# Row sums of a 64 MB tensor: the last row in a tile of its own, its first part's sum passed on as an element and not as a start value

## The chip, the cores and the metric

The kernel runs on one core of one Trainium2 chip. The metric is device microseconds of one execution. Every run that is told here is marked as fast in the record, with a granted clock (the share of the full clock that the chip allowed) of 1.0.

## The reference

```python
def setup_inputs():
    batch, seq, dim = 32, 512, 1024
    return {
        "x": np.random.randn(batch, seq, dim).astype(np.float32),
        "multiplier": 0.5,
    }

def reference(x, multiplier):
    return (np.sum(x, axis=-1) * multiplier).astype(np.float32)
```

There are 16384 rows of 1024 fp32 numbers, 67.11 MB in all. Each row becomes one number.

## The kernel before

The 128 partitions take 128 rows each. Seven blocks of 16 rows per partition are loaded whole, 8 MB at a time; the last block comes in pieces of 8, 5 and 2 rows, and its last row in two parts of 576 and 448 elements. This keeps the work that must follow the last byte small. In the last block, VectorE adds one half of a row to the other and sums as it goes, so that the size of such a sum is counted in pairs of elements. In the seven blocks before, it reduces whole rows and multiplies the results by 0.5. ScalarE takes some of the rows.

```python
    part = res_pool.tile([P, 1], fp32, name="part")
    # ...
    def dve_span(t, r, lo, hi, dst, start=0.0):
        mid = (lo + hi) // 2
        return nc.vector.tensor_tensor_reduce(
            out=t[:, r, lo:mid],
            in0=t[:, r, lo:mid],
            in1=t[:, r, mid:hi],
            scale=mul,
            scalar=start,          # the sum starts from this
            op0=ADD,
            op1=ADD,
            accum_out=dst,
        )
    # ... the last row of the last block
    for lo, hi in ((0, cut), (cut, D)):          # cut = 576, D = 1024
        loads.append(nc.sync.dma_start(
            out=t[:, B - 1, lo:hi], in_=x_last[:, B - 1, lo:hi]))
    # ...
    first = dve_span(t, B - 1, 0, cut, part)
    part_seen = nop_after(nc.vector, [first], [])     # waits until part is written
    final = dve_span(t, B - 1, cut, D, res[:, rows - 1 : rows], start=part)
    # ... store of the last 16 results of each partition, which waits for final
```

The sum of the first part goes into `part`, one number per partition. The sum of the second part starts from it. Two things must be true before that second sum may start: its load has landed, and `part` is written. The first wait is in the instruction; the second has a no-op of its own in front.

## Time and profile before

| | before |
|---|---|
| time, median of 3 runs | 161.98 us (161.96 to 161.98) |
| span of the trace | 160.2 us |
| transfer engines, busy | 97.4% |
| VectorE, busy | 74% |
| last load landed | 157.467 us |
| last sum, from start to end | 157.551 to 158.001 us |

The table is to be read from its third line: the transfers are the limit, and only what comes after the last landing is in the hands of the compute engines. The prediction shows the lines. Times to the nanosecond, here and below, are from the trace's records of instructions and of semaphore counts; 0 is the start of the span. A semaphore is a counter that instructions wait for, and the count of a load is complete when its sixteenth increment is there. In the profile's lines DVE is VectorE, DVEq its queue, SPq the queue that issues the transfers, and CUSTOM_DVE_ANT_0 the fused add and sum.

### The profile page before, as it was taken

Reading aid. Unit: us, or ns where it says so; the run is one execution under the profiler, and the core shown is the slowest. Engines: PE = TensorE matmul, PEld = TensorE weight load, DVE = VectorE, ACT = ScalarE, POOL = GpSimd, SP = SyncE. Lnnn points to the kernel's source line nnn. Section 1 sums busy time; section 2 is a strip of 40 time slices with the busy share of each in tenths; the row PEclk is TensorE's granted clock in tenths of the full one; section 3 lists DMA queues with packets and bytes.
Section 4 is the critical chain, followed back from the end, with each engine's and each line's share of the span. In section 5 each row is a group of like instructions: output and inputs, shape, how many; then the busy total and the mean of one; then the engine's idle time right before and its main releaser. Section 6 shows DMA issues by size and latency. Waiting matters only on the chain.

```text
span 160.2 us, 138 instructions
## 1 busy us (share of the span) xinstructions
DVE 119.3 (74%) x34; ACT 17.3 (11%) x31; POOL 0.2 (0%) x4
## 2 busy tenths in 40 slices
DVE  0000059997799969999599995999959999597443
ACT  0000000000000000000000000000000000599952
POOL 0000000000000000000000000000000000000000
DMA  7996996996996996997997998979969969999992
GB/s 278 507 524 262 524 524 262 524 524 262 524 524 262 524 524 262 524 475 311 524 442 344 524 409 376 524 311 475 524 278 507 524 278 507 393 393 425 430 399 72
DMA packets 2016, 67.18 MB, mean 419 GB/s; under 512 B 480, under 2 KB 608, under 8 KB 736
## 3 DMA queue, kind: packets, MB, share of 16 engines
q1 hardware_dynamic: 2016, 67.18, 97.4%
HBM read 67.11 MB, written 0.07 MB: 419 GB/s over the span
## 4 chain that ended last, share of the span: by engine, by line
DMA 75%; DVE 22%; SPq 1%; issue 0%; DVEq 0%
DMA xb<-in_x_dram 75%; DVE sums L96 22%; SPq L114 1%; DVE xb L80 0%; SPq L120 0%; SPq L94 0%; DVE res L99 0%; DVEq L205 0%
## 5 line engine op out<-in xcount | busy, mean ns | idle before, releaser
L96 DVE TENSOR_REDUCE sums<-xb 128x16 f32<-128x16384 f32 (+1 forms) x7 | 112.0, 16001 | 33.3 <-DMA xb<-in_x_dram 33.3
L70 ACT ACT_TABLE_LOAD x1 | 1.3, 1283 | 137.9 <-DMA xb<-in_x_dram 137.9
L70 ACT ACTIVATE xb<-xb 128x1024 f32<-128x1024 f32 x15 | 15.7, 1045 | 2.1 <-DMA xb<-in_x_dram 2.1
L80 DVE CUSTOM_DVE_ANT_0 xb<-xb 128x512 f32<-128x512 f32 (+1 forms) x9 | 5.6, 664 | 5.0 <-DMA xb<-in_x_dram 5.0
L70 ACT ACTIVATION_READ_ACCUMULATOR xb<-xb 128x1 f32 x15 | 2.8, 187 | 0.0
L99 DVE TENSOR_SCALAR res<-sums 128x16 f32<-128x16 f32 (+1 forms) x7 | 1.2, 174 | 0.2
L80 DVE DVE_READ_ACCUMULATOR2_ANT res<- 128x1 f32 x9 | 0.7, 83 | 0.0
L80 DVE CUSTOM_DVE_ANT_0 xb<-xb,part 128x224 f32<-128x224 f32 x1 | 0.5, 450 | 0.2 <-DMA xb<-in_x_dram 0.2
L191 POOL MEMSET const-bfloat16-1.0<- 128x1 bf16 x1 | 0.1, 101 | 0.0
L191 POOL MEMSET const-uint8-127<- 128x1 uint8 x1 | 0.1, 101 | 0.0
L191 POOL MEMSET const-float32-0.0<- 128x1 f32 x1 | 0.1, 98 | 0.2 <-issue 0.2
L191 POOL MEMSET const-float32-1.0<- 128x1 f32 x1 | 0.1, 98 | 0.0
L80 DVE DVE_READ_ACCUMULATOR2_ANT part<- 128x1 f32 x1 | 0.1, 83 | 0.0
## 6 DMA issues: line engine op xcount, KB each, us to landing
xb<-in_x_dram SPq DMA_DIRECT2D x1, 4096.0 KB, 31.1
xb<-in_x_dram SPq DMA_DIRECT2D x1, 2560.0 KB, 36.9
xb<-in_x_dram SPq DMA_DIRECT2D x1, 1024.0 KB, 38.9
xb<-in_x_dram SPq DMA_DIRECT2D x1, 288.0 KB, 39.1
xb<-in_x_dram SPq DMA_DIRECT2D x1, 224.0 KB, 39.2
xb<-in_x_dram SPq DMA_DIRECT2D x7, 40.8
out_dram<-res SPq DMA_DIRECT2D x1, 56.0 KB, 10.0
out_dram<-res SPq DMA_DIRECT2D x1, 8.0 KB, 1.4
```

The source lines that it names most:

```text
L70: acts.append(nc.scalar.activation(out=t[:, r, :], in_=t[:, r, :], func=mybir.ActivationFunctionType.Copy, scale=mul, accum_out=res[:, col ...
L80: return nc.vector.tensor_tensor_reduce(out=t[:, r, lo:mid], in0=t[:, r, lo:mid], in1=t[:, r, mid:hi], scale=mul, scalar=start, op0=ADD, o ...
L96: nc.vector.reduce_sum(out=sums[:, c0 : c0 + h], in_=t[:, 0:h, :], axis=mybir.AxisListType.X)
L99: nc.vector.tensor_single_scalar(out=res[:, c0 : c0 + h], in_=sums[:, c0 : c0 + h], scalar=mul, op=mybir.AluOpType.mult,)
L114: nc.sync.dma_start(out=t[:, lo:hi, :], in_=x_last[:, lo:hi, :])
L191: nc = _bacc.Bacc("TRN2", target_bir_lowering=False, num_devices=1)
```

## The change

It means to take a memory operand off the last instruction. The last row lands in a tile `end`, in which its two parts lie apart. The sum of the first part is written into the element just before the second part. With a zero in front of it (so that the count stays even) the second sum takes it in as one more element, and starts from the 0.0 that stands in the instruction. The first sum is no longer multiplied by 0.5 (its scale is 1.0), since the second one scales all that it takes in. The diff is shortened.

```diff
-    part = res_pool.tile([P, 1], fp32, name="part")
+    cut = 576
+    at = 608
+    end = res_pool.tile([P, at + D - cut], fp32, name="end")
+    nc.vector.memset(end[:, at - 2 : at], 0.0)
...
-    def dve_span(t, r, lo, hi, dst, start=0.0):
+    def dve_sum(row, dst, scale):          # always scalar=0.0
...
-    for lo, hi in ((0, cut), (cut, D)):
+    for to, lo, hi in ((0, 0, cut), (at, cut, D)):
         loads.append(
             nc.sync.dma_start(
-                out=t[:, B - 1, lo:hi], in_=x_last[:, B - 1, lo:hi]
+                out=end[:, to : to + hi - lo], in_=x_last[:, B - 1, lo:hi]
             )
         )
...
-    first = dve_span(t, B - 1, 0, cut, part)
+    first = dve_sum(end[:, 0:cut], end[:, at - 1 : at], 1.0)
     part_seen = nop_after(nc.vector, [first], [])
-    final = dve_span(t, B - 1, cut, D, res[:, rows - 1 : rows], start=part)
+    final = dve_sum(end[:, at - 2 :], res[:, rows - 1 : rows], mul)
```

## The prediction

> **What bounds the kernel now.** I read the views in this order: the busy row of the page, its DMA row and queue row, the chain that ended last in order of time, the timeline of VectorE at the end, and the same group of instructions by shape.
>
> First the page, to see whether an engine or the transfers set the time:
>
> ```profile
> span 160.2 us, 138 instructions
> DVE 119.3 (74%) x34; ACT 17.3 (11%) x31; POOL 0.2 (0%) x4
> ...
> q1 hardware_dynamic: 2016, 67.18, 97.4%
> HBM read 67.11 MB, written 0.07 MB: 419 GB/s over the span
> ```
>
> The 16 transfer engines are busy 97.4% of the span. The kernel is a stream of 67 MB from HBM, and VectorE (74%) and ScalarE (11%) work in its shade. An edit that leaves the bytes and their order alone can only act on what lies before the first byte or after the last one. So the second view is the end of the chain in order of time (columns: start us, us, what):
>
> ```profile
> 117.76 0.43 SPq L120
> 118.19 0.04 issue
> 118.24 39.23 DMA xb<-in_x_dram
> 157.47 0.08 issue
> 157.55 0.45 DVE xb L80
> 158.00 0.01 DVEq L205
> ```
>
> The last load (the second part of the last row, elements 576 to 1023) lands at 118.24 + 39.23 = 157.47. It was issued at 118.2, some 39 us earlier, and stood in the queue behind blocks 5, 6 and the rest of the last block. After it come 0.08 us of waiting, 0.45 us of VectorE and the end. The third view is the timeline of those last VectorE instructions and the last store (start us, us, engine, line, operation):
>
> ```profile
> 156.93 0.46 DVE L80 CUSTOM_DVE_ANT_0 xb<-xb 128x288 f32<-128x288 f32 x1
> 157.32 0.08 DVE L80 DVE_READ_ACCUMULATOR2_ANT part<- 128x1 f32 x1
> 157.55 0.45 DVE L80 CUSTOM_DVE_ANT_0 xb<-xb,part 128x224 f32<-128x224 f32 x1 [0.15 <-DMA xb<-in_x_dram]
> 157.93 0.08 DVE L80 DVE_READ_ACCUMULATOR2_ANT res<- 128x1 f32 x1
> 158.04 0.34 SPq L142 DMA_DIRECT2D out_dram<-res  x1
> ```
>
> The tail is: landing 157.47, sum of the second part 157.55 to 158.00, its accumulator out at 158.01, store issued at 158.04 and landed 1.4 us later, the closing barrier to 160.2. Everything after 157.55 is serial. The measured 161.98 us is 1.8 us over the span, outside what any instruction touches.
>
> The fourth view, by shape, holds the oddity on which the change rests:
>
> ```profile
> L80 DVE CUSTOM_DVE_ANT_0 xb<-xb 128x512 f32<-128x512 f32 x8 | 5.1, 690 | 5.0 <-DMA xb<-in_x_dram 5.0
> L80 DVE CUSTOM_DVE_ANT_0 xb<-xb 128x288 f32<-128x288 f32 x1 | 0.5, 459 | 0.1
> L80 DVE CUSTOM_DVE_ANT_0 xb<-xb,part 128x224 f32<-128x224 f32 x1 | 0.5, 450 | 0.2 <-DMA xb<-in_x_dram 0.2
> ```
>
> From 512 to 288 element pairs, 224 fewer, the same instruction loses 231 ns, 1.03 ns each. From 288 to 224, 64 fewer, it loses only 9 ns where 66 were due. The last one is about 57 ns too long for its size, and it is the only one that takes its start value from memory (`part`, one value per partition) and not from the instruction.
>
> **What the Trainium skill says.** "VectorE: DVE Perf Modes", section "The TRN2 errata", gives (N+151)/0.96 ns for an fp32 two-tensor add. The trace agrees for both sizes without `part`: 691 against 690 measured, 457 against 459. For 224 it gives 391 where 450 was measured, so the excess is 59 ns by this count. "DVE: scalar operands, raw-bit mode, write accounting and state across instructions", section "Scalar operands", says that such a one-per-partition operand is read and converted on load; it gives no price, and the trace of before suggests one of 57 to 59 ns inside the duration. "VectorE: DVE Perf Modes", section "The DRAIN you can't avoid", says that a value just written by VectorE is read stale by the next VectorE instruction unless a semaphore, or an instruction in between, separates them. That is why the no-op with a wait stays in the change; in the trace it is a 21 ns event on VectorE's queue at 157.4.
>
> **The change part by part.** I compared the instruction order of both built kernels, with their waits.
>
> 1. *A memset of two elements of the new tile*, first on VectorE. It comes long before the first row block lands: VectorE stands idle to 21.78 us in the timeline. Beside other work, 0 on the path. The loads into the new tile carry no wait on it.
>
> 2. *The last row lands in a tile of its own.* The two loads keep their place in the queue (after the three other pieces), their bytes (288 and 224 KB) and their 128 runs of 2304 and 1792 bytes. They lose no wait, because before they carried none of their own: they only stand behind the piece that waits for the buffer. The last load thus lands when it did, 157.47: 0 us.
>
> 3. *The first part's sum*: 288 pairs as before, 459 ns, scale 1.0 instead of 0.5, accumulator read of 83 ns to another address: 0 us.
>
> 4. *The no-op*: the same wait on the same instruction: 0 us.
>
> 5. *The second part's sum*: 225 pairs instead of 224 (+1 ns), start value from the instruction. By the formula (225+151)/0.96 = 392 ns; by the line through the two measured sizes, 459 - 63 x 1.03 = 394 ns. Against 450 this saves 56 to 58 ns. It is wholly on the path: accumulator, store and barrier move up by as much. Take -57 ns.
>
> 6. *The start of that sum.* It begins 0.08 us after the landing. The other four sums that waited for a load begin about 24 ns after the last count of its semaphore (for the first part, 156.908 to 156.932 in the trace's semaphore records). So 60 ns are unexplained there. Either the per-partition operand delays the start as well (then they go, -60 ns more), or the no-op does: it ends at 157.46, and the sum starts 92 ns after it, which can be the time in which VectorE's queue takes the next instruction in. The queue of SP takes some 63 ns from one wait to the next in the same window, so I find the no-op the likelier one, about two to one. Expected: one third of -60, -20 ns, though most likely 0.
>
> Sum: -57 - 20 = -77 ns as a mean, -57 ns most likely. 161.98 - 0.07 = 161.91 us.
>
> **The rivals.** (a) *The start moves up as well.* For it: 84 ns from landing to start against 24 elsewhere, and only this sum has the operand. Against: the no-op ends only 8 ns before the landing and would explain the gap alone. It makes 161.86. (b) *The saving is not there*: the 57 ns belong to something else of the last sum, such as reading bytes that landed a moment ago, or the odd start of the new operands (elements 606 and 831 of the tile, the earlier ones at multiples of 32) costs as much as it saves. For it: one single instruction is all the evidence for the price. Against: the sums of 512 and 288 also read right after a landing and fit the formula to 2 ns. It makes 161.98 to 162.0. (c) *The tile of its own lets its loads start early*, since no buffer must come free for them, and the last bytes are then others. Against: the built order keeps them last on SP's queue, behind a piece that waits; and the transfers are busy 97.4% of the time, so an earlier start could only change the order of the bytes and not their sum. It makes no difference. (d) *The landing moves*, because destinations in another tile are written at another rate or the stream falls otherwise on the engines. For it: 39 us of queued transfers stand before it, and 0.1% of the stream is 0.16 us, more than the whole expected gain. Against: the runs are as long as before, and the three times of before lie within 0.02 us. It makes 161.8 to 162.1.
>
> **Range and chances.** Most likely 161.92 from step 5 alone, 161.86 with rival (a), 161.98 or a little above with (b), and (d) spreads each by about 0.1. I say 161.91, with 161.78 to 162.04 as the range for 8 in 10. A move of 2% is 3.2 us; nothing on the whole tail after the last landing (157.47 to 160.2, 2.7 us) is as long, so only a fault of the stream could bring it: 1% on each side.
>
> **What would show each step right or wrong.** Right: the last sum, now 128x225, shows 390 to 396 ns; its accumulator read stays near 83; the last load lands at 157.5 within 0.1; the busy row and the queue's share stay as they are. For step 6: if the gap from landing to start stays near 0.08, the no-op holds it; if it falls towards 0.02, the operand did. Wrong: a duration of 440 or more for the last sum (then the operand was not the cost), a landing that moved by over 0.1 us (then the difference is the stream's, and the sum says nothing about it), or a wait of SP or VectorE near the start of the run that was not there before, which would mean that the memset or the new tile holds a load.

## The result, and the profile after

| | before | after |
|---|---|---|
| time, median of 6 runs each in the same rounds | 162.01 us (161.96 to 162.19) | 161.99 us (161.93 to 162.07) |
| ratio | | 0.9997, 95% interval 0.9984 to 1.001 |
| span of the trace | 160.2 us | 160.2 us |
| last load landed | 157.467 us | 157.518 us |
| no-op ended | 157.459 us | 157.520 us |
| last sum started | 157.551 us | 157.610 us |
| last sum took | 450 ns | 394 ns |
| last sum ended | 158.001 us | 158.004 us |
| from landing to the end of the sum | 534 ns | 486 ns |

A ratio is the mean time of one kernel's fast runs over that of the other's of the same rounds, so it is not quite the ratio of the medians quoted beside it. The prediction (161.91, range 161.78 to 162.04) was right.

The first lines of the page of the kernel after: its instructions are one more (the memset), and the rest is all but unchanged (the queue's share was 97.4%).

```profile
span 160.2 us, 139 instructions
DVE 119.3 (74%) x35; ACT 17.3 (11%) x31; POOL 0.2 (0%) x4
...
q1 hardware_dynamic: 2016, 67.18, 97.6%
```

The groups by shape of the kernel after (busy us, mean ns of one, idle before):

```profile
L84 DVE CUSTOM_DVE_ANT_0 xb<-xb 128x512 f32<-128x512 f32 x8 | 5.1, 688 | 5.0 <-DMA xb<-in_x_dram 5.0
...
L84 DVE CUSTOM_DVE_ANT_0 end<-end 128x288 f32<-128x288 f32 x1 | 0.5, 458 | 0.1
L84 DVE CUSTOM_DVE_ANT_0 end<-end 128x225 f32<-128x225 f32 x1 | 0.4, 394 | 0.1
```

The last sum took 450 ns before. Now, with one pair more, it takes 394 and lies on the line of the other two sizes. That is the change at work, as it was meant. The chain of the kernel after, at its end (start us, us, what), shows why the total hardly moved:

```profile
117.89 39.08 DMA end<-in_x_dram
156.97 0.02 issue
156.99 0.48 DVE end L84 x2
157.47 0.03 issue
157.50 0.02 DVEq L63
157.52 0.09 issue
157.61 0.39 DVE end L84
158.00 0.01 DVEq L208
```

The sum is 0.06 us shorter, yet it ends at 158.00, as before. The chain has another form: it no longer goes back from the last sum to the second part's landing, but to the no-op (`DVEq L63`), from there to the first part's sum (at 156.99), and from there to the first part's landing at 156.97. (In the kernel before, the chain names the landing, which came 8 ns after the end of the no-op; the experiments show that the no-op set the start there too.) Everything in it stands some 0.06 us later than before, because the first part landed at 156.970 and not at 156.908. The timeline of VectorE near the start shows that about this much of a delay was there long before the last row. This is the first row block's sum, first of the kernel before:

```profile
21.78 17.22 DVE L96 TENSOR_REDUCE sums<-xb 128x16 f32<-128x16384 f32 x1 [21.78 <-DMA xb<-in_x_dram]
```

and this the memset and the same sum in the kernel after:

```profile
1.81 0.06 DVE L55 MEMSET end<- 128x2 f32 x1 [1.81 <-PEq L194]
21.83 17.22 DVE L100 TENSOR_REDUCE sums<-xb 128x16 f32<-128x16384 f32 x1 [19.96 <-DMA xb<-in_x_dram]
```

The first load landed 49 ns later in the profiled run of the kernel after (21.804 against 21.755), and the last load 51 ns later. The saving of the end and the lateness of the stream were of one size in this pair of traces. In the times the means of the six runs each differ by 0.047 us (162.037 and 161.990), less than what one run scatters.

### The profile page after: what moved, and what is told of

The parts are those of the page before. It is cut to its first block, busy times and chain, and to the rows that moved or that the text cites. A ratio compares the mean times of both kernels' runs of the same rounds, so it can differ in the third digit from the quotient of the medians.

```text
span 160.2 us, 139 instructions
## 1 busy us (share of the span) xinstructions
DVE 119.3 (74%) x35; ACT 17.3 (11%) x31; POOL 0.2 (0%) x4
## 4 chain that ended last, share of the span: by engine, by line
DMA 75%; DVE 22%; SPq 1%; issue 0%; DVEq 0%
DMA xb<-in_x_dram 51%; DMA end<-in_x_dram 24%; DVE sums L100 22%; SPq L117 1%; DVE end L84 1%; SPq L98 0%; DVE res L103 0%; DVEq L63 0%; DVEq L208 0%
## 5 line engine op out<-in xcount | busy, mean ns | idle before, releaser
L84 DVE CUSTOM_DVE_ANT_0 xb<-xb 128x512 f32<-128x512 f32 x8 | 5.1, 688 | 5.0 <-DMA xb<-in_x_dram 5.0
L84 DVE CUSTOM_DVE_ANT_0 end<-end 128x288 f32<-128x288 f32 (+1 forms) x2 | 0.9, 426 | 0.2
```

What stands on the lines that cost most here:

```text
L84: return nc.vector.tensor_tensor_reduce(out=row[:, 0:mid], in0=row[:, 0:mid], in1=row[:, mid:], scale=scale, scalar=0.0, op0=ADD, op1=ADD, ...
```

## The experiments

The theory: the memory operand costs the sum some 58 ns inside its duration and nothing before its start; the start is held by whichever is later, the landing or the no-op. Rival A: the operand also delays the start. Rival B: the excess of 450 ns belongs to the tile or to bytes just landed, and not to the operand. Rival C: the tile of its own makes the stream later, which ate the gain. Eleven runs were made, in three groups; each group shares its runs of the kernel before. The groups ran on three different chips. The diffs are shortened.

### The operand alone: taken away in the old layout, put back in the new one

`e1_start_imm` is the kernel before with one word changed. Its output is wrong, which doesn't matter for the time.

```diff
-    final = dve_span(t, B - 1, cut, D, res[:, rows - 1 : rows], start=part)
+    final = dve_span(t, B - 1, cut, D, res[:, rows - 1 : rows], start=0.0)
```

> The kernel before, but the last sum starts from the 0.0 in its instruction and not from the first part's sum; one value in 128 is then wrong, on purpose. Theory (the memory operand costs 57 to 59 ns inside the sum, and the no-op holds its start): the last 128x224 sum takes 391 to 394 ns in place of 450, and it starts 90 to 92 ns after the end of the no-op, as before. Rival A (the operand also delays the start): the start comes 24 to 40 ns after the landing or after the no-op. Rival B (the excess belongs to the tile or to bytes just landed): it stays at 450 ns. Time by the theory 0.06 us below before, within the noise of 0.1.

`e2_start_zero` is the kernel after with a start value of zero from memory.

```diff
+    zero = res_pool.tile([P, 1], fp32, name="zero")
+    nc.vector.memset(zero, 0.0)
-    final = dve_sum(end[:, at - 2 :], res[:, rows - 1 : rows], mul)
+    final = dve_sum(end[:, at - 2 :], res[:, rows - 1 : rows], mul, start=zero)
```

> The changed kernel with the last sum's start value 0.0 read from a one-per-partition tile of zeros. Theory: the 128x225 sum takes 450 to 453 ns in place of 394; start again 90 to 92 ns after the no-op. Rival B (the own tile or the layout made it short): it stays at 394. Time by the theory as the kernel before, 0 to 0.1 us above the changed one.

The last sum by shape in `e1_start_imm`:

```profile
L80 DVE CUSTOM_DVE_ANT_0 xb<-xb 128x224 f32<-128x224 f32 x1 | 0.4, 393 | 0.1
```

and in `e2_start_zero`:

```profile
L86 DVE CUSTOM_DVE_ANT_0 end<-end,zero 128x225 f32<-128x225 f32 x1 | 0.5, 453 | 0.2 <-DMA end<-in_x_dram 0.2
```

In the old layout the sum falls from 450 to 393 ns without the operand; in the new layout it rises from 394 to 453 with it. The operand costs 57 ns in one and 59 in the other, whatever the tile. In e2 the value had been in memory since the start of the run, so the price is not one of a value just written. Rival B falls. The start stays where the no-op puts it: 90 ns after its end in e1 (157.475 to 157.565), 92 in e2 (157.561 to 157.653). The times say nothing, as expected: 162.07 and 162.10 us beside 162.10 for the kernel before (ratios 0.9998 and 0.9999).

### The operand seventeen times over

Sixteen more sums of the same shape stand between the no-op and the last sum, with results in scratch. They differ in the start value alone: read from the tile of zeros, or in the instruction.

```diff
+    more = res_pool.tile([P, 16], fp32, name="more")
+    for k in range(16):
+        row, lo = k % 4, 240 * (k // 4)
+        extra = dve_sum(end[:, at - 2 :], more[:, k : k + 1], mul,
+                        start=zero,        # 0.0 in e4_more16_imm
+                        to=t[:, row, lo : lo + 225])
```

(The last sum itself has 0.0 in the instruction in both, so the difference is of sixteen operands. In both traces a single no-op waits for the first part's sum and for the landing: the first of the sixteen starts 170 and 169 ns after the landing, which is 92 and 91 ns after the end of the no-op.)

> The changed kernel with sixteen more sums of the same 225 pairs between the no-op and the last sum, each into scratch, each with a start value of 0.0 read from a tile of zeros. Against the next kernel, the same with 0.0 in the instruction. Theory: each costs 57 to 59 ns more than there, so the time is 0.91 to 0.95 us above the next kernel's, and both are 5 to 7 us over the changed kernel. If the operand is read while the sum before it still runs, the difference falls to under 0.3 us; if it delays the start as well, it is 1.5 us or more.

> The changed kernel with sixteen more sums of 225 pairs, each with 0.0 in the instruction. Theory: back to back each takes some 320 to 400 ns from start to start, so 5 to 7 us over the changed kernel; each lasts 392 to 395 ns by itself.

By shape, the sixteen in `e3_more16_ptr`:

```profile
L86 DVE CUSTOM_DVE_ANT_0 xb<-end,zero 128x225 f32<-128x225 f32 x16 | 6.1, 450 | 0.2 <-DMA end<-in_x_dram 0.2
```

and in `e4_more16_imm`:

```profile
L86 DVE CUSTOM_DVE_ANT_0 xb<-end 128x225 f32<-128x225 f32 x16 | 5.1, 391 | 0.3 <-DMA end<-in_x_dram 0.3
```

Back to back they start every 375 ns with the operand and every 314 without (a little under the 320 to 400 that were expected): 61 ns each. From the landing to the end of the last sum it is 6683 against 5710 ns, and 973 / 16 is 61. The medians are 168.27 us (5 runs) and 167.31 us (4 runs), a difference of 0.96 us or 60 ns per operand, just over the 0.91 to 0.95 us that were expected; the means differ by 1.03 us, as one of the four times (167.12) is low. This is the change's mechanism in a size that the time can show: what is taken off this tail comes off the time in full, and the operand's price isn't hidden behind the sum before. The traces agree: from the end of the last sum to the end of the span it is 2.207 to 2.216 us in all thirteen. The longer price that rival A would give (1.5 us or more in all) did not come.

### The no-op off the path: cut at 480

A smaller first part is summed earlier, so the no-op is done before the second part lands. If the operand delays the start, that delay must now stand alone.

```diff
-    cut = 576
+    cut = 480
```

> The kernel before with the last row cut at element 480 and not 576, so that the first part's sum and the no-op behind it are done well before the second part lands. The start value still comes from memory. Theory (the no-op alone holds the start): the last sum starts 24 ns after the landing, in place of 84; with 272 pairs it takes 441 + 58, so 496 to 502 ns. Rival A (the operand delays the start): it starts 80 to 90 ns after the landing although the no-op is done. Time: 60 ns less of gap, 50 ns more of sum, so as before.

> The changed kernel, cut at 480. Theory: start 24 ns after the landing, 273 pairs in 440 to 444 ns. From the landing to the end of the sum 466, against 486 in the changed kernel.

The end of the chain in `e5_cut480_ptr` (the kernel before, cut at 480):

```profile
118.48 39.17 DMA xb<-in_x_dram
157.65 0.03 issue
157.67 0.50 DVE xb L80
158.18 0.01 DVEq L205
```

and in `e6_cut480_imm` (the changed kernel, cut at 480):

```profile
118.28 39.19 DMA end<-in_x_dram
157.47 0.02 issue
157.49 0.44 DVE end L84
157.93 0.01 DVEq L208
```

With the operand the sum starts 25 ns after the landing, without it 23. In the kernel before it was 84 ns. So the operand does not delay the start: rival A falls, and the no-op was what held it. The sums took 502 ns (272 pairs) and 443 (273 pairs), 59 apart. From landing to end it is 527 ns with the operand, 466 without. In time: 162.03 and 161.93 us, beside 162.13 for the kernel before (ratios 0.9994 and 0.9988, both intervals hold 1).

### The changed kernel again

> The changed kernel once more, for the scatter of the landing. Theory: the last sum takes 394 ns again and starts 90 ns after the no-op; the landing lies anywhere in 157.4 to 157.6, so the time is within 0.1 us of the kernel before. Rival (the tile of its own makes the stream slower): the landing is later than that of before by 50 ns or more again.

The last sum took 393 ns and started 90 ns after the no-op; from landing to end it was 488 ns. The last load landed at 157.504. Its median was 162.12 us beside 162.13. The landings of the last load in all traces of cuts at 576 without further sums were 157.467 (before) and 157.489 (e1) into the row block's tile, and 157.518 (after), 157.504 (e8) and 157.555 (e2) into the tile of its own. With the sixteen further sums they were 157.591 and 157.624, in the tile of its own. So at this cut every landing in the own tile was later than both in the old one. The traces with other cuts, above and below, do not bear that out: they go from 157.419 (own tile) to 157.679 (own tile), with 157.543 and 157.648 for the old tile between, and the mean of all traces is 157.54 for either tile. The first load alone landed anywhere from 21.66 to 22.00 us. From its landing to that of the last load it took 135.645 to 135.729 us in the four traces of the old tile, and 135.653 to 135.825 in eight of the nine of the own tile (136.021 in e7), with medians of 135.698 and 135.714. A price of the tile itself, rival C, is not visible in this, though one of a few tens of ns is not excluded; a scatter of a quarter of a microsecond in the landing is visible, and it is several times what the change is worth. Why the landing scatters was not pursued.

### A cut that gets both gains: 544

A cut at 544 should let the no-op end just in time and keep the last sum shorter than the cut at 480 does.

```diff
-    cut = 576
+    cut = 544
```

> The changed kernel, cut at 544: a candidate that takes the no-op just off the path and keeps the last sum short. Theory: start 24 to 40 ns after the landing, 241 pairs in 408 to 412 ns; from landing to the end of the sum 435 to 450 ns, against 486 in the changed kernel and 534 in the one before. The time should be 0.04 us under the changed kernel and 0.1 us under the one before, if the landing stays; its scatter of 0.1 us may hide that.

> The cut at 544 in the changed kernel once more, to see whether its 0.10 us at the end of the trace (435 ns from landing to the end of the last sum, against 534 in the kernel before) can be seen in the time. Theory: 435 ns again; time 0.1 us (ratio 0.9994) under the kernel before. If the time follows the landing alone, the ratio is 1.0000 within the scatter.

> The same kernel a third time, for five more times: 435 ns from landing to the end of the last sum, ratio 0.9994.

> The kernel before, cut at 544, the start value still from memory. Theory (operand and no-op are two separate costs): 240 pairs with the operand take 466 to 469 ns, start 24 to 30 ns after the landing, so 490 to 499 ns from landing to the end, as much as the change alone gains (486) by the other way; ratio 0.9997.

The end of the chain in `e10_cut544_more`:

```profile
118.28 39.14 DMA end<-in_x_dram
157.42 0.02 issue
157.44 0.41 DVE end L84
157.85 0.01 DVEq L208
```

and in `e11_cut544_ptr`, the kernel before with this cut:

```profile
118.36 39.18 DMA xb<-in_x_dram
157.54 0.04 issue
157.58 0.47 DVE xb L80
158.05 0.01 DVEq L205
```

All the tails, in order of what they take after the landing (us from the start of the span; the sum and the last column in ns):

| run | cut | start value | landed | no-op ended | sum started | sum | landing to end |
|---|---|---|---|---|---|---|---|
| e10 | 544 | instruction | 157.419 | 157.343 | 157.442 | 411 | 434 |
| e7 | 544 | instruction | 157.679 | 157.603 | 157.703 | 411 | 435 |
| e9 | 544 | instruction | 157.471 | 157.410 | 157.501 | 411 | 441 |
| e6 | 480 | instruction | 157.467 | 157.313 | 157.490 | 443 | 466 |
| e1 | 576 | instruction | 157.489 | 157.475 | 157.565 | 393 | 469 |
| after | 576 | instruction | 157.518 | 157.520 | 157.610 | 394 | 486 |
| e8 | 576 | instruction | 157.504 | 157.509 | 157.599 | 393 | 488 |
| e11 | 544 | memory | 157.543 | 157.489 | 157.581 | 467 | 505 |
| e5 | 480 | memory | 157.648 | 157.490 | 157.673 | 502 | 527 |
| before | 576 | memory | 157.467 | 157.459 | 157.551 | 450 | 534 |
| e2 | 576 | memory | 157.555 | 157.561 | 157.653 | 453 | 551 |

One rule holds in all eleven rows: the sum starts at the later of two times, the landing plus 23 to 25 ns, or the end of the no-op plus 90 to 92 ns. e11 missed its expectation by 6 ns (505 against 490 to 499) for the same reason: its two parts landed only 587 ns apart, so the no-op came last by a little. e9 was held by 6 ns in the same way. In e3 and e4, where both waits were in the no-op, the second time alone counted.

The cut at 544 in the changed kernel saves 93 to 100 ns at the end against the kernel before. One set of five times doesn't show this: the three medians were 162.09, 162.01 and 161.96 us beside 162.13, 162.04 and 162.04 (ratios 0.9993, 0.9996 and 0.9993, each interval holds 1; the last two share their runs of the kernel before). Together, the mean of the 15 is 161.997 us, and the mean of the 18 of the kernel before in the same rounds is 162.096. The difference of 0.098 us has a standard error of 0.035, worked out from the scatter of the single runs (0.108 and 0.091 us). It agrees with the trace, and it is 0.06%. The rounds of e9 and e10 give 0.086 us by themselves, and those of e7 0.104. Times of this size do not rank the cuts: e6, with a tail longer by 25 to 32 ns, had the lowest median of all (161.93 us). That 544 is the better cut is read from the tails alone. The old form at this cut (e11) took 162.06 us, ratio 0.9998.

## Why the prediction was right, point by point

- **Step 1, the memset: 0.** Right. It took 60 ns at 1.81 us, while VectorE waited for the first block.
- **Step 2, the loads: 0, landing at 157.47.** Right within the 0.1 us that the text allowed. The landing came at 157.518, and 49 of the 51 ns were there at the first load, before anything that the change touches at its end. The landings of the other runs show no price of the new tile.
- **Steps 3 and 4, first sum and no-op: 0.** Right: 458 ns against 459, no-op of 21 ns in both.
- **Step 5, the last sum: 392 to 394 ns, -56 to -58.** Right: 394 in the profile, and the operand's price measured by itself is 57 ns (e1) and 59 (e2), or 61 in the spacing of sums back to back. The view by shape was enough for this, because one instruction was out of line with two others of its kind.
- **Step 6, the start: -20 as a mean, 0 most likely.** The term was mis-sized; its true size is 0. The favoured reading of the two was right: the no-op held the start, 92 ns before the sum in the kernel before and 90 in the changed one. The 60 ns that looked unexplained are on the path, but they belong to the no-op, and the cuts at 480 and 544 took all or most of them away (23 to 38 ns from landing to start).
- **The sum, -77 ns.** Too large by the -20 of step 6 (and carried on as -0.07 us, where it rounds to -0.08). From landing to the end of the sum the profile shows -48: -56 of the sum itself, and 8 more from landing to start (92 against 84), because the no-op ended 8 ns before the landing in the one trace and 2 ns after it in the other. The time moved by -0.047 us as a mean of six against six, which agrees but would not prove it.
- **The rivals.** (a) fell with e5. (b) fell with e1 and e2; the odd start of the new operands costs next to nothing (394 ns for 225 pairs, against 393 for 224 with even starts in e1). (c): the order of the loads stayed, as foreseen. (d) is what the times show: the scatter of the stream is larger than the gain, and it set the width of the range rightly. But the range held 161.98 as well, the time with no gain at all: that 161.99 fell inside it is no test of the mechanism; the traces are. Of the 0.08 us between 161.91 and 161.99, 0.03 are in the kernel before, which took 162.01 us in these rounds and 161.98 in those on which the prediction rests.

In the tail the gain is thus there, and the sixteen-fold test shows that such a gain reaches the time in full. It is about 0.03% of the time; in six times against six it stays below the scatter.

## What to carry to other kernels

When a kernel is bound by its transfers, price the few instructions that follow the last landing, one by one: here each nanosecond counted in full there. Look for an instruction that is out of line with others of its kind by size; here a start value read from memory cost 57 to 61 ns. A wait with a no-op of its own put 90 to 92 ns in front of the next sum, where a wait in the sum itself put 23 to 25; it costs about as much, and can be moved off the path by choosing where the data is cut. Before a gain of 0.05% is claimed or denied, multiply the suspected cost until the clock can see it.

## What the Trainium skill lacked or had wrong

- "DVE: scalar operands, raw-bit mode, write accounting and state across instructions", section "Scalar operands", gives no price for an operand of one value per partition. For this fused add and sum it was 57 ns (450 against 393) and 59 ns (453 against 394) in the duration, and 61 ns per instruction in a row of sixteen (375 against 314 from start to start). Other operations were not tried.
- "VectorE: DVE Perf Modes", section "The TRN2 errata", gives (N+151)/0.96 ns for a plain fp32 add of two tensors. It holds for this fused form as well where no such operand is read: 394 against 392 for 225 pairs, 411 against 408 for 241, 443 against 442 for 273, 690 against 691 for 512.
- "VectorE: DVE Perf Modes", section "The DRAIN you can't avoid", says of a chain of copies that "the semaphore costs nothing extra here". It has no figure for a wait that is an instruction of its own. Here the next sum started 90 to 92 ns after such a no-op ended, but 23 to 25 ns after the count when the wait stood in the sum itself and the no-op had ended at least 99 ns before the start. Where the wait for the landing was in the no-op too (e3 and e4), the sum started 170 and 169 ns after the count.
